# q and k of a head in transfers of 64 and 128 rows, and another order of ScalarE's queue before attention

## The chip, the cores and the metric

The kernel runs on one core of one Trainium2 chip. A core has four engines that compute, each with its own in-order queue: TensorE (PE in the profile, with its weight loads as PEld), VectorE (DVE), ScalarE (ACT) and GpSimd (POOL). A fifth, SyncE (SP), does nothing here but issue transfers. Transfers run on 16 DMA engines beside all of them. ACT and POOL issue some transfers too, and an engine that waits with an issue also holds up what stands behind it in its queue.

The metric is the device time of one execution in microseconds. The kernel before took 2428.34 us, the median of three runs (2427.61 to 2428.85).

## The reference

One decoder layer on x of 4096 x 1024, in float32: an RMS norm, an input projection, two groups of heads, gates, an output projection and a second norm.

```python
h = rms_norm(x, norm_gain)
qa, ka, va, ga, qr, kr, vr, gr = split(h @ w_in)
attn = dilated_attention(qa, ka, va)   # 8 heads of 64, branches (128,1), (512,4), (2048,16)
ret = retention(qr, kr, vr)            # 4 heads, key 64, value 128, chunks of 128
x = x + concat(silu(ga) * attn, silu(gr) * ret * ret_gn_gain) @ w_out
return rms_norm(x, final_gain)
```

Each attention head looks at its keys three times, with stride 1, 4 and 16, and merges the three results by their softmax denominators. q and k are rotated by their positions first.

## The kernel before, in words

It has three phases. **Phase 1** goes through x in eight blocks of 512 positions. For each block PE computes the projections in groups: q0, q1, k0, k1 (four heads of attention each), r0, r1 (retention's q and k), then the values. Every product is split in three matmuls (`mm3`) of high and low parts. A group gives two PSUM banks, A and B; there are seven such banks (`p1mm`). `rotate` turns them on DVE into two tiles `o` (tag `o`, two buffers), ACT and DVE split each into a tile `hl` (two buffers), and SP stores it to the DRAM tensors `dr["q"]`, `dr["k"]` or `dr["r"]`. In `dr["q"]` and `dr["k"]`, of shape [2, 2, 8, 32, 4096], the first index says whether the row is a high or a low part, the second which half of the 64 dimensions it belongs to, the third is the head. `store_values` scales a value bank on ACT into `vo` (two buffers) and ACT issues six transfers of it to `dr["v"]`, where the values lie in three orders, one for each stride.

In the last block the order is r0, r1, q0, q1, k0, k1. After r1 the function `make_room` loads the first head's q for its first 2048 positions (`load_q`, half 0). After k0, and before k1 is rotated, SP gets the load of x's first chunk of 128 positions (`load_x_chunk`) and the load of the first head's k but for the last 512 positions (`load_k`); after k1's rotation the rest of k. Then ACT's queue holds, in this order: the split of the first x chunk (`split_h_chunk`, ACT copies and POOL subtracts), eight splits of the weights w2 (`ahead["w2"].split`), and four times `store_values`. SP's queue has the load of the second x chunk after the second k load; it uses the same buffer as the first.

**Phase 2** is attention, with the retention and its values as filler. PE's order is fixed by hand: each head has 24 groups of four blocks of 128 queries, two steps a group, so 384 steps in all. Every step issues scores (`qk_bank`), transposes, products with v (`pv_group`) and copies of the results; between them the generator `filler` puts pieces of the retention, so many that a planned number of ns is filled. `LEAD` is the filler that comes before the first step. The groups of a head come in the order: stride 1 in the first half of the positions (4 groups), stride 4 (8), stride 16 (8), stride 1 in the second half (4). `gather_q` copies q of the strided groups together four steps ahead, part 0 on POOL and part 1 on DVE.

q lies in four tiles per head: high or low part (i), and first or second half of the positions. Each holds its 64 rows twice, in rows 0 to 63 and 64 to 127. k lies in one tile of 128 rows per head, in two pools that alternate. A head's k is loaded in the head before, from its group 6 on, its first half of q from group 20 on, its second half when the head begins. These loads go through a list, `pending`; `issue_due` sends of it at every step as many as a number `room` allows. Tiles of results have three buffers (`p2os`), their stores are issued two steps after the copy. v comes in tiles of 1024 positions, six buffers, two tiles ahead.

**Phase 3** has the gates, the output projection and the last norm, and is not touched.

Two lines that the steps below refer to: the cos and sin tables of phase 1 are loaded into 128 rows from 32 (L181), and rotated r is stored with the heads as the outermost index (L249):

```python
nc.sync.dma_start(tab[:, i, :], io[nm][:, b * BLK : (b + 1) * BLK].unsqueeze(0).broadcast_to([4, 32, BLK]))
nc.sync.dma_start(dr["r"][idx, :, part, :, cols], o)
```

Of the kernel before, what the change touches and what calls it, by code (L numbers as in the profile page):

```python
# [8 lines left out]
F32 = mybir.dt.float32  # L9
# [19 lines left out]
BLK = 512  # L29
NBLK = S // BLK  # L30
# [85 lines left out]
def phase1(tc, io, dr, right, ahead):  # L116
# [3 lines left out]
    nc = tc.nc  # L120
    gain, rs = ahead["gain"], ahead["rs"]
    with ExitStack() as ctx:
# [5 lines left out]
        op = ctx.enter_context(tc.tile_pool(name="p1o", bufs=2))  # L128
# [16 lines left out]
        for g in ("r", "k", "q", "v"):  # L145
            p = {"v": wp, "q": wpool}.get(g) or right.open(f"p1w{g}")
            i = "qkrv".index(g)
# [6 lines left out]
                tag="w" if g == "q" else None,  # L154
                room=[(qp[0], "q00"), (qp[0], "q10")] if g == "r" else None,
# [22 lines left out]
        def load_tables(b, n):  # L178
            tab = tp.tile([128, 2, BLK], F32, tag=f"tab{n}", name=f"tab{n}1")
            for i, nm in enumerate((f"cos{n}", f"sin{n}")):  # L180
                nc.sync.dma_start(tab[:, i, :], io[nm][:, b * BLK : (b + 1) * BLK].unsqueeze(0).broadcast_to([4, 32, BLK]))  # L181
            return tab
# [33 lines left out]
        def scaled(tab, rb):  # L216
            for i in range(2):
                nc.gpsimd.tensor_tensor(tab[:, i, :], tab[:, i, :], rb, ALU.mult)

        def products(g, i, hs, p, ks=range(KT)):  # L220

            for k in ks:
                mm3(
                    nc,
                    p,
                    [(*W[g].at(k, slice(i * 128, i * 128 + 128)), hs[k][:, 0, :], hs[k][:, 1, :])],
                    k == 0,
                    k == KT - 1,
                )

        def bank():
            return pmm.tile([128, BLK], F32, tag="mm", name="mm1")
# [34 lines left out]

        def store_values(b, i, p):
            n = 4 * b + i
            vf = op.tile([128, 512], F32, tag="vo", name="vo1")  # L270
            nc.scalar.activation(vf, p, AF.Copy, scale=rs[:, n : n + 1])

            nc.scalar.dma_start(dr["v"][0, n * 128 : (n + 1) * 128].rearrange("(r l) e -> l r e", r=16), vf)

            r0 = (n // 16) * 128 + (n % 16) * 8
            nc.scalar.dma_start(dr["v"][2].rearrange("(r q) e -> q r e", q=256)[r0 : r0 + 8], vf)

            for r in range(4):
                r0 = r * 1024 + b * 128 + i * 32
                nc.scalar.dma_start(dr["v"][1, r0 : r0 + 32].rearrange("(a l) e -> l a e", a=4), vf[r:128:4, :])  # L280
# [42 lines left out]
        for b in range(NBLK):  # L323
            last = b + 1 == NBLK
            names = "RA" if last else "AR"
            tabs = {"A": tabA, "R": tabR}
            if b:
                tabs[names[0]] = load_tables(b, names[0])
            xts, hnext, waiting = [], [], []
            for gi, (g, half) in enumerate(LASTG if last else GROUPS):  # L330
                if b == 0 and g == "q":
                    ps = first[2 * half : 2 * half + 2]
                else:
                    ps = [bank() for _ in range(2)]
                    for part in range(2):
                        products(g, 2 * half + part, hcur, ps[part])
                        if b and gi == 0 and part == 0:
                            diag = root(b)
                if gi == (0 if b else 2):
                    rb = along_free(b, diag)  # L340
                    scaled(tabs[names[0]], rb)
                    if b:
                        tabs[names[1]] = load_tables(b, names[1])
                        scaled(tabs[names[1]], rb)
                waiting.append((g, half, ps))

                while len(waiting) > 1 and rb is not None:
                    w, x, (A, B) = waiting.pop(0)
                    rotate(b, w, x, A, B, tabs["R" if w == "r" else "A"])
                if b == 0 and gi == 1:  # L350
                    for k in range(KT):
                        W["r"].split(k, nc.gpsimd if k % 2 else None)
                if b == 0 and gi == 3:
                    scaled(tabR, rb)
                    for k in range(KT):
                        W["v"].split(k, nc.gpsimd if k % 2 else None)
                if not last and gi >= 3:
                    while len(xts) < (2, 3, 4)[gi - 3]:
                        xts.append(load_xt(b + 1, len(xts)))
                    if gi == 4:  # L360
                        hnext.append(make_h(b + 1, 0, xts[0]))
                if last:
                    make_room(gi)
            if last:
                right.close(2)
                qp[1] = right.open("p2q1")
                hcp, kka = ahead["hcp"], ahead["kka"] = right.open("p2h"), right.open("p2ka")
                raw = load_x_chunk(nc, hcp, io, 0)
                kk = load_k(nc, kka, dr, 0, cols=slice(0, S - BLK))
                w, x, (A, B) = waiting.pop(0)  # L370
                rotate(b, w, x, A, B, tabs["A"])
                ahead["kk"] = load_k(nc, kka, dr, 0, cols=slice(S - BLK, S), t=kk)
                ahead["hch"] = {0: [split_h_chunk(nc, hcp, raw, 0, i) for i in range(2)]}
                ahead["hr"] = load_x_chunk(nc, hcp, io, 1)
                for k in range(KT):
                    ahead["w2"].split(k)
                for i in range(4):
                    p = bank()
                    for k in range(KT):
                        values(b, i, k, hcur, p)  # L380
                    store_values(b, i, p)
            else:
                pv = [bank() for _ in range(4)]
                for k in range(KT):
                    for i in range(4):
                        values(b, i, k, hcur, pv[i])
                    if k == 0:
                        w, x, (A, B) = waiting.pop(0)
                        rotate(b, w, x, A, B, tabs["R"])
                    if k + 1 < KT:  # L390
                        hnext.append(make_h(b + 1, k + 1, xts[k + 1]))
                    if len(xts) < KT:
                        xts.append(load_xt(b + 1, len(xts)))
                for i in range(4):
                    store_values(b, i, pv[i])
                hcur = hnext
# [22 lines left out]
def load_x_chunk(nc, pool, io, c):  # L419
    t = pool.tile([128, KT, 128], F32, tag="hr", name="hr2")  # L420
    nc.sync.dma_start(t, by_blocks(io["xT"])[:, :, c * 128 : (c + 1) * 128])
    return t


def split_h_chunk(nc, pool, t, c, i):

    hc = pool.tile([128, KT // 2, 2, 128], F32R, tag=f"hc{(2 * c + i) % 3}", name="hc2")
    src = t[:, KT // 2 * i : KT // 2 * (i + 1), :]
    nc.scalar.activation(hc[:, :, 0, :], src, AF.Copy)  # L429
    nc.gpsimd.tensor_tensor(hc[:, :, 1, :], src, hc[:, :, 0, :].bitcast(F32), ALU.subtract)  # L430
    return hc


def load_k(nc, pool, dr, h, dma=None, cols=slice(0, S), t=None):
    dma = dma or nc.sync.dma_start
    t = t or pool.tile([128, S], F32R, tag="kk", name="kk2")
    for i in range(2):
        for part in range(2):
            p0 = i * 64 + part * 32
            dma(t[p0 : p0 + 32, cols].bitcast(F32), dr["k"][i, part, h, :, cols])  # L440
    return t


# [61 lines left out]
def load_q(nc, pool, dr, h, i, half, dma=None):  # L505
    dma = dma or nc.sync.dma_start
    t = pool[half].tile([128, S // 2], F32R, tag=f"q{i}{half}", name=f"q2_{i}{half}")
    for dup in range(2):
        for part in range(2):
            p0 = dup * 64 + part * 32  # L510
            dma(t[p0 : p0 + 32, :].bitcast(F32), dr["q"][i, part, h, :, half * 2048 : (half + 1) * 2048])
    return t


def phase2(tc, io, dr, right, ahead, early3, raw, M):

    nc = tc.nc
    W2, hcp, kka, qp = (ahead[n] for n in ("w2", "hcp", "kka", "qp"))
    with ExitStack() as ctx:
# [47 lines left out]
        def issue_due():  # L567
            for fn, args in delayed.pop(clock[0], []):
                fn(*args)
            room = 250  # L570
            while pending and room > 0:
                dst, src = pending.pop(0)
                nc.sync.dma_start(dst, src)
                room -= dst.shape[0] * dst.shape[1] // 512

        pending = []

# [275 lines left out]
        hch, hraw = ahead["hch"], {1: ahead["hr"]}  # L853
# [555 lines left out]
```

## Time and profile before

| what | us |
|---|---|
| median of the three runs | 2428.34 |
| the profiled execution | 2426.76 |
| its span, first to last instruction | 2425.0 |
| phase 1 up to PE's last matmul before its hole | 761.86 |
| that hole of PE | 22.37 |
| attention's scores, first to last | 789.3 to 1657.0 |

In the profile's rows a line number follows the engine; `dst<-src` names tiles and tensors. SPq and ACTq are issues of transfers, not the transfers themselves; `[14.45 <-DMA x]` behind a row is the engine's idle time before it and what ended it. Issues of transfers in between are not counted as work, so an idle time on ACT can hold six of them. A row of windows has the length, then each engine's busy time with its number of instructions, the granted TensorE clock, the share of the 16 DMA engines' time that was busy, and the GB/s they moved. In the chain of work that ended last, a DMA row's length is the time from issue to landing.

### The profile page before, as it was taken

What the parts mean: (1) busy time and instruction counts of PE and PEld (TensorE: products, weight loads), DVE (VectorE), ACT (ScalarE), POOL (GpSimd) and SP (SyncE); (2) the same over time, 40 slices, a digit from 0 to 9 for tenths busy, and PEclk for the clock granted to TensorE, in tenths of its full rate; (3) what the DMA queues carried; (4) which work ended last, traced back from release to release, by engine and by line L of the source; (5) the groups of instructions that cost most, each with busy time, mean ns of one, the idle gap of its engine ahead of it and who ended that gap; (6) DMA issues with size and microseconds to landing.
All of it is one profiled execution on the core that took longest, in us unless ns stands there. A gap on an engine that the chain in (4) does not pass through costs nothing.

```text
span 2425.0 us, 41805 instructions
## 1 busy us (share of the span) xinstructions
PE 2339.9 (96%) x14568; PEld 1984.7 (82%) x14568; DVE 1486.3 (61%) x3921; ACT 992.1 (41%) x2868; POOL 721.8 (30%) x761
## 2 busy tenths in 40 slices
PE   7999999999996999999999999996899999999998
PEld 5778888888885888888888888875789999999997
DVE  5643543543432878787887879786655565565554
ACT  4322212212202666667666666666222232222221
POOL 5312112112112535353543535444221121121110
PEclk9999999999998999999999999998999999999999
DMA  6343343343356665757575665745665656666563
GB/s 191 130 144 112 127 143 114 125 143 123 118 161 187 163 162 138 182 130 192 130 178 150 164 157 135 181 137 169 154 159 166 142 159 163 144 164 156 141 155 92
DMA packets 404259, 362.59 MB, mean 150 GB/s; under 512 B 191848, under 2 KB 334824, under 8 KB 398928
## 3 DMA queue, kind: packets, MB, share of 16 engines
q1 hardware_dynamic: 389408, 332.91, 51.6%
q10 hardware_dynamic: 14112, 25.43, 3.4%
q8 instruction: 115, 1.88, 0.3%
q0 software_dynamic: 528, 1.58, 0.2%
q14 instruction: 96, 0.79, 0.1%
HBM read 241.18 MB, written 118.64 MB: 148 GB/s over the span
## 4 chain that ended last, share of the span: by engine, by line
PE 81%; DMA 6%; DVE 4%; ACT 2%; issue 1%; POOL 1%; ACTq 1%; SPq 1%; POOLq 0%; DVEq 0%
PE S L640 9%; PE O L710 7%; PE mm L50 7%; PE mm L49 7%; PE mm L51 7%; PE T L677 6%; PE po L50 4%; PE po L51 4%; PE po L49 4%; PE g L50 4%; PE g L49 4%; PE g L51 4%; PE V L49 3%; PE V L51 2%; PE V L50 2%; DMA wb<-dr_w 1%
## 5 line engine op out<-in xcount | busy, mean ns | idle before, releaser
L661 DVE CUSTOM_DVE_ANT_0 S<-S,mask 128x256 f32<-128x256 f32 (+1 forms) x768 | 308.4, 402 | 154.4 <-PE S L640 115.7
L668 ACT ACTIVATE P<-S,nm 128x256 f32<-128x256 f32 (+1 forms) x768 | 337.3, 449 | 44.4 <-DVE nm L661 41.1
L51 PE MATMUL g<-h,wg 128*128 128x256 f32 x1024 | 290.4, 284 | 0.0
L677 PE MATMUL T<-ident,P 128*128 128x128 f32 x1368 | 213.1, 273 | 0.5 <-ACT P L668 0.4
L50 PE MATMUL po<-wo,m 128*128 128x512 f32 x512 | 201.5, 394 | 0.0
L51 PEld LDWEIGHTS g<-h,wg 128*128 128x128 f32 x1024 | 197.5, 193 | 0.1
L710 PE MATMUL O<-pt,v 128*64 128x128 f32 (+1 forms) x1968 | 196.1, 325 | 0.2 <-ACT pt L687 0.2
L640 PE MATMUL S<-kk,qc 128*128 128x256 f32 x1024 | 186.5, 305 | 5.7 <-issue 2.6
L1202 POOL TENSOR_TENSOR rs<-v,mhalf 128x1 f32<-128x1 f32 x32 | 17.3, 540 | 554.5 <-DVE v L1200 554.5
L640 PEld LDWEIGHTS S<-kk,qc 128*128 128x128 f32 x1024 | 149.2, 190 | 33.5 <-issue 17.0
L51 PE MATMUL po<-wohi,m 128*128 128x512 f32 x448 | 176.3, 394 | 0.0
L49 PE MATMUL po<-wohi,m 128*128 128x512 f32 x448 | 174.8, 390 | 0.9 <-DVE x L1195 0.9
L173 POOL TENSOR_TENSOR sq<-sq,sq 128x512 f32<-128x512 f32 x56 | 76.3, 1362 | 331.4 <-ACT sq L169 331.4
L430 POOL TENSOR_TENSOR hc<-hr,hc 128x512 fp32r<-128x512 f32 x64 | 85.9, 1344 | 293.7 <-ACT hc L429 210.7
L710 PEld LDWEIGHTS O<-pt,v 128*64 128x64 f32 x1968 | 121.3, 136 | 60.7 <-issue 31.5
L677 PEld LDWEIGHTS T<-ident,P 128*128 128x128 f32 x1368 | 163.6, 141 | 1.1 <-ACT P L668 1.1
L49 PE MATMUL g<-h,wg1hi 128*128 128x256 f32 x512 | 146.0, 286 | 13.7 <-ACT h L464 13.7
L668 ACT ACTIVATION_READ_ACCUMULATOR P<-S,nm 128x1 f32 x768 | 157.5, 205 | 0.0
L41 ACT ACTIVATE m<-e 128x256 fp32r<-128x256 f32 x128 | 53.3, 417 | 240.8 <-DVE e L1148 140.9
L50 PE MATMUL g<-h,wg1hi 128*128 128x256 f32 x512 | 148.1, 289 | 3.8 <-DVE h L465 3.3
L49 PE MATMUL g<-h,wg0hi 128*128 128x256 f32 x512 | 145.0, 283 | 4.7 <-ACT e L1141 4.7
L1141 ACT ACTIVATE e<-g 128x256 f32<-128x256 f32 x128 | 48.3, 378 | 237.1 <-PE g L51 233.4
(207 smaller groups left out, 6207.5 us busy)
## 6 DMA issues: line engine op xcount, KB each, us to landing
q<-dr_q SPq DMA_DIRECT2D x128, 256.0 KB
hr<-in_xT_dram SPq DMA_DIRECT2D x64, 512.0 KB
wb<-dr_w SPq DMA_DIRECT2D x128, 192.0 KB
o<-dr_o SPq DMA_DIRECT2D x192, 128.0 KB
v<-dr_v SPq DMA_DIRECT2D x94, 256.0 KB
xt<-in_xT_dram SPq DMA_DIRECT2D x64, 256.0 KB
dr_q<-hl SPq DMA_DIRECT2D x32, 512.0 KB
dr_k<-hl SPq DMA_DIRECT2D x32, 512.0 KB
```

The lines of the kernel that those rows point to most:

```text
L41: nc.scalar.activation(dst[:, 0], src, AF.Copy)
L49: nc.tensor.matmul(out, wh, xh, start=first and i == 0, stop=False)
L50: nc.tensor.matmul(out, wh, xl, start=False, stop=False)
L51: nc.tensor.matmul(out, wl, xh, start=False, stop=last and i == n - 1)
L173: nc.gpsimd.tensor_tensor(sums[b], sums[b], sq, ALU.add)
L430: nc.gpsimd.tensor_tensor(hc[:, :, 1, :], src, hc[:, :, 0, :].bitcast(F32), ALU.subtract)
L640: nc.tensor.matmul(s[:, j * 256 : (j + 1) * 256], qq[h, t, half][:, off : off + 128] if br == 0 else it["q"][:, t, i, :], rhs, start=(j == ...
L661: nc.vector.tensor_tensor_reduce(sv, sv, mask[:, it["br"], c0:256], 1.0, BIG, ALU.add, ALU.min, accum_out=nm[:, col : col + 1])
L668: nc.scalar.activation(it["P", i // 2][:, i % 2, c0:256], sv, AF.Exp, bias=nm[:, col : col + 1], scale=-1.0, accum_out=den[:, col : col + 1])
L677: nc.tensor.transpose(t[:, j * 128 : (j + 1) * 128], it["P", bank][:, j // 2, j % 2 * 128 : j % 2 * 128 + 128], ident)
L710: nc.tensor.matmul(o[64 * bank : 64 * bank + 64, c0 : c0 + 128 * m], vt[h, br, idx // 8][:, idx % 8, :], it["pt"][:, a : a + m, :].rearran ...
L1141: nc.scalar.activation(e, g, AF.Silu)
```

## The change

Three things. `load_k` issues one transfer of 128 rows instead of four of 32, and `load_q` two transfers of 64 rows per tile instead of four of 32; the number that `issue_due` takes off `room` for a transfer is halved per element to fit. At the passage the first x chunk is split, and the second loaded, after the first of the last block's four `store_values` and no longer before the w2 splits. And the third and fourth of these `store_values` take a buffer of the tag `hl` instead of `vo`.

```diff
         def store_values(b, i, p):
             n = 4 * b + i
-            vf = op.tile([128, 512], F32, tag="vo", name="vo1")
+            if b + 1 == NBLK and i >= 2:
+                vf = op.tile([128, 2, BLK], F32, tag="hl", name="vo1")[:, 0, :]
+            else:
+                vf = op.tile([128, 512], F32, tag="vo", name="vo1")
             nc.scalar.activation(vf, p, AF.Copy, scale=rs[:, n : n + 1])
...
                 ahead["kk"] = load_k(nc, kka, dr, 0, cols=slice(S - BLK, S), t=kk)
-                ahead["hch"] = {0: [split_h_chunk(nc, hcp, raw, 0, i) for i in range(2)]}
-                ahead["hr"] = load_x_chunk(nc, hcp, io, 1)
                 for k in range(KT):
                     ahead["w2"].split(k)
                 for i in range(4):
@@
                         values(b, i, k, hcur, p)
                     store_values(b, i, p)
+                    if i == 0:
+                        ahead["hch"] = {0: [split_h_chunk(nc, hcp, raw, 0, j) for j in range(2)]}
+                        ahead["hr"] = load_x_chunk(nc, hcp, io, 1)
...
 def load_k(nc, pool, dr, h, dma=None, cols=slice(0, S), t=None):
     dma = dma or nc.sync.dma_start
     t = t or pool.tile([128, S], F32R, tag="kk", name="kk2")
-    for i in range(2):
-        for part in range(2):
-            p0 = i * 64 + part * 32
-            dma(t[p0 : p0 + 32, cols].bitcast(F32), dr["k"][i, part, h, :, cols])
+    dma(t[:, cols].bitcast(F32), dr["k"][:, :, h, :, cols].rearrange("i t d s -> (i t) d s"))
     return t
...
     for dup in range(2):
-        for part in range(2):
-            p0 = dup * 64 + part * 32
-            dma(t[p0 : p0 + 32, :].bitcast(F32), dr["q"][i, part, h, :, half * 2048 : (half + 1) * 2048])
+        p0 = dup * 64
+        dma(t[p0 : p0 + 64, :].bitcast(F32), dr["q"][i, :, h, :, half * 2048 : (half + 1) * 2048])
     return t
...
                 nc.sync.dma_start(dst, src)
-                room -= dst.shape[0] * dst.shape[1] // 512
+                room -= dst.shape[0] * dst.shape[1] // 1024
```

## The prediction, made before the changed kernel was run

> **What bounds the kernel now.** I read the page first, for the busy shares, the queues and the issues:
>
> ```profile
> PE 2339.9 (96%) x14568; PEld 1984.7 (82%) x14568; DVE 1486.3 (61%) x3921; ACT 992.1 (41%) x2868; POOL 721.8 (30%) x761
> ...
> q1 hardware_dynamic: 389408, 332.91, 51.6%
> ...
> q<-dr_q SPq DMA_DIRECT2D x128, 256.0 KB
> ...
> kk<-dr_k SPq DMA_DIRECT2D x28, 512.0 KB
> ```
>
> PE is busy for 96% of the span. The transfers fill half of the DMA engines' time, so they cost nothing as long as each lands before its reader. The change is about them and about one hole, so I read the windows of attention, of the passage to it and of the 3.4 us behind it:
>
> ```profile
> 790.00:1660.00 870.00, 858.81 (x6744) 719.41 (x6742) 698.48 (x2572) 600.58 (x2063) 401.41 (x450) 1.00 0.64 156
> 762.00:784.20 22.20, 0.00 (x0) 0.00 (x0) 0.87 (x3) 2.60 (x5) 3.85 (x6) 0.61 0.68 234
> 784.20:787.60 3.40, 3.37 (x10) 2.65 (x11) 0.00 (x0) 0.50 (x1) 3.33 (x4) 0.51 0.04 11
> ```
>
> The columns are length, busy time of PE, PEld, DVE, ACT and POOL, granted clock, DMA share, GB/s. In attention PE is busy for 858.8 of 870 us at full clock. At the passage it does nothing for 22.2 us and then runs 3.4 us at a clock of 0.51: a long hole costs 3.4 x 0.5 = 1.7 us more. The timeline of PE and ACT names the hole's end:
>
> ```profile
> 743.01 1.15 ACT L429 ACTIVATE hc<-hr 128x512 fp32r<-128x512 f32 x2 [3.27 <-DMA hr<-in_xT_dram]
> 744.07 4.39 ACT L84 ACTIVATE w2hi<-w,gain_all 128x512 fp32r<-128x512 f32 x7
> ...
> 767.84 0.69 ACT L271 ACTIVATE vo<-mm,rs_all 128x512 f32<-128x512 f32 x1 [4.75 <-DMA dr_v<-vo]
> ...
> 774.69 4.78 ACTq L280 DMA_DIRECT2D dr_v<-vo  x4
> 782.97 0.63 ACT L429 ACTIVATE hc<-hr 128x512 fp32r<-128x512 f32 x1 [14.45 <-DMA dr_v<-vo]
> 783.51 0.67 ACT L1009 ACTIVATE vch<-V,rs_all 128x512 f32<-128x512 f32 x1
> ...
> 784.23 0.80 PE L49 MATMUL V<-w2hi,hc 128*128 128x512 f32 x1 [22.37 <-ACT vch L1009]
> ```
>
> PE waits for vch, which stands in ACT's queue behind the last v store's transfers and a split (hc) that needs the second chunk of x.
>
> **How many engines a transfer runs on.** This decides the case. Two SP rows and six windows, in which hardly anything but the transfer named was in flight:
>
> ```profile
> 686.68 0.55 SPq L181 DMA_DIRECT2D tabA<-in_cosA_dram  x1
> ...
> 703.11 1.56 SPq L249 DMA_DIRECT2D dr_r<-o  x2
> ...
> 666.00:669.00 3.00, 3.00 (x14) 2.45 (x13) 0.00 (x0) 0.00 (x0) 0.00 (x0) 1.00 0.47 124
> 688.00:691.40 3.40, 3.40 (x16) 2.78 (x15) 2.84 (x6) 0.00 (x0) 0.95 (x1) 1.00 0.23 73
> 710.20:712.30 2.10, 2.10 (x11) 1.71 (x10) 0.00 (x0) 0.00 (x0) 0.00 (x0) 1.00 0.26 101
> 720.00:729.00 9.00, 9.00 (x40) 7.29 (x40) 6.74 (x11) 1.27 (x2) 0.00 (x0) 1.00 1.01 335
> 744.80:748.40 3.60, 3.60 (x18) 2.98 (x17) 3.28 (x4) 3.60 (x7) 1.92 (x2) 1.00 0.20 50
> 794.00:801.00 7.00, 7.00 (x56) 5.77 (x55) 5.92 (x24) 5.14 (x16) 3.54 (x4) 1.00 1.00 213
> ```
>
> A share of 1.00 is 16 engines. At 720 to 729 the w2 loads run (128 rows on both sides): all 16. At 794 to 801 the q loads of today (32 rows on both sides): all 16, though at 213 GB/s, not 335. At 666 to 669 the v stores, whose DRAM side is cut into 8 outermost pieces (L273 to L280): 0.47, about 8 engines. At 710 to 712 only the dr_r stores of L249, whose DRAM side has 4 heads outermost: 0.26, 4 engines. At 688 to 691 only the tabA loads, whose source is broadcast with 4 copies outermost (L181): 0.23, again 4. So a transfer uses as many engines as its outermost count on either side allows. The new k load has 4 pieces outermost ((i t) d s): 4 engines. The new q load has 2 (part, d, s): 2 engines. No row shows a 2; that it gives 2 continues 16, 8, 4.
>
> The Trainium skill, "DMA: Bandwidth & Descriptors", section "Why a DMA increments its semaphore by 16 and not by 1", says that a transfer's engines are the largest number up to 16 that divides the slowest dimension of both patterns; by it q gets 2 and k 4, and the sum is the one below. By that rule the 8 and the 4 of the windows agree; what it says of a 2 no run here shows yet, and four engines for q stay a rival.
>
> Rate of one engine, GB/s over 16 x share: 24.3 (dr_r), 19.8 (tabA), 15.6 (744.8 to 748.4, the tail of the kk loads on some three engines), 13.3 (q today). I take 17.7, the mean of the two rows that load SBUF with few engines; the ends are 24.3 and 13.3.
> - q transfer: 64 x 8 KB = 524,288 bytes, half on each engine: 262,144 / 17.7 = **14.8 us** (10.8; 19.7). Today 256 KB at 213 GB/s take 1.2.
> - k load: 128 x 16 KB, a quarter each: 524,288 / 17.7 = **29.6 us** (21.6; 39.4).
>
> **The change part by part.** Rows for the time there is:
>
> ```profile
> 790.63 3.70 SPq L573 DMA_DIRECT2D q<-dr_q  x8
> 803.86 1.50 POOL L616 CAST qc<-q 128x512 fp32r<-128x512 f32 x1
> ...
> 1092.46 2.78 SPq L573 DMA_DIRECT2D q<-dr_q  x6
> 1128.27 0.64 DVE L616 CAST qc<-q 128x512 fp32r<-128x512 f32 x1 [0.19 <-DMA q<-dr_q]
> 1092.40:1128.20 35.80, 35.60 (x290) 30.10 (x286) 26.37 (x101) 25.47 (x88) 11.73 (x13) 1.00 0.86 209
> ...
> L640 PE MATMUL S<-kk,q x512: 274/281/392, 789.3 to 1657.0; 128*128 128x256 f32 x171
> ...
> 718.20 4.26 DMA dr_q<-hl
> ```
>
> *q, from one head to the next.* The next head's first half is loaded from 1092.46 on, its second half from 1113, and the gather at 1128.27 needs the second: 36 us, already 0.19 us late. The second half's tiles are read by the old head's last groups, so the two halves come one after the other, and all eight transfers use the same two engines: 8 x 14.8 = 118. Beside it the other transfers' share of these engines: 0.86 x 35.8 = 30.8 us less 4.19 MB of q at 213 GB/s = 19.7 leaves 11. One hand-over, from issue to landing with little in front, is 4 (4.26 us). So 118 + 11 + 4 - 36 = **+97** (65; 137); nothing hides it, since PE has no idle time to give. Seven times: +680 (455; 959). For the first head the second half alone: 4 x 14.8 + 4 - 13 (790.63 to 803.86) = **+50** (34; 70).
>
> *k.* A step of attention is 867.7 us / 384 = 2.26. The k load goes out some 2 steps before the next store of O. O has three buffers, and one is wanted again 4 steps after its store's issue: 6 x 2.26 = 13.6 us after the k load. The store's part on the four engines stands behind k: 29.6 + 4 - 13.6 = **+20** each (12; 30), ACT waiting first and PE behind it. Seven times +140 (84; 210).
>
> *room // 1024.* Still two q transfers a step, but of twice the bytes, and one k. It sends them at most two steps (4.5 us) sooner into engines that are behind already: nothing.
>
> *The passage.* Rows:
>
> ```profile
> 693.38 10.72 DMA q<-dr_q
> 704.16 10.71 DMA dr_r<-o
> 712.49 0.69 DVE L241 TENSOR_TENSOR o<-mm,tabA 128x512 f32<-128x512 f32 x1 [8.80 <-DMA dr_r<-o]
> 734.48 0.39 PE L49 MATMUL mm<-w1vhi,h 128*128 128x512 f32 x1
> 733.33 1.56 SPq L260 DMA_DIRECT2D dr_k<-hl  x2
> 735.54 20.62 SPq L440 DMA_DIRECT2D kk<-dr_k  x4
> ```
>
> The first head's q loads stand in front of the last dr_r stores: today one such store takes 10.71 us instead of the 2.6 that 256 KB need at 101 GB/s, and q's rotation waits for it. Now 4 x 14.8 = 59 us from about 698, then two stores of 2.7: landed at 763 instead of 712.4, **+51**. PE holds 7 PSUM banks, stops before the second bank of the last k group (734.48 - 24 x 0.233 = 728.9) and goes on 37 us later. The k stores move from 733.3 to 784, landing at 786; the first k load (448 KB an engine) takes 26, its tail and hand-over 6, the second chunk of x stands behind it on these engines: about 820, and vch 822 instead of 783.5: **+38** (15; 68, with 10.8 and 19.7).
>
> ACT's new order puts the eight w2 splits before the hc splits: they need not wait until 743.01, 744.8 instead of 749.1 for the first v store; the two hc copies (1.15 us) and the load of the next chunk on SP follow that store. SP's own order stays (the second k load, then the chunk), POOL's subtraction has nothing queued behind it but the constants. The hl buffers for the third and fourth chunk free them of the earlier v stores; they wait for the last k stores instead, and behind them on ACT stand their transfers, hc and vch. With k that late this gains and costs nothing; without the q and k loads it would be worth 15 us (next part).
>
> *Clock.* Three holes a head and two at the passage, 23 x 1.7 = +39.
>
> Sum: 680 + 50 + 140 + 38 + 39 = **+947** (+627; +1346). The profiled execution took 2426.76 us, span 2425.0; the median shown is 1.6 above it. 2428 + 947 = **3375**; with the ends 3055 and 3775.
>
> **The rivals.**
> - *Sixteen engines all the same* (faster). If the count that matters were the rows in SBUF, the loads would get quicker (toward 335 GB/s) and only the passage would move: vch follows the fourth v store. The first comes at 744.8, each holds ACT for some 5.4 us (its 0.7 and six issues, 4.7 in the row of 767.84), hc takes 1.2 in between and 0.6 at the end: vch at 768 instead of 783.5, -15, **2412**. For it: today's 32-row loads get 213 GB/s where 128 rows get 335. Against it: 0.23 for tabA, whose SBUF side has 128 rows. It decides if the q loads' share of the DMA is 1. The Trainium skill, "DMA: Bandwidth & Descriptors", section "Rules for kernel authors", advises one 128-partition transfer in place of two on halves, and read alone that speaks for this rival; the trace doesn't bear it out for tabA, a 128-partition transfer on a quarter of the engines.
> - *Four engines for q too.* 7.4 us a transfer: 7 x (59 + 11 + 4 - 36 = 38) + 21 + 140 + 8 + 39 = +474: **2900**. Against it: 16, 8 and 4 follow the count.
> - *The two q engines hinder each other* and get 13.3 (today's 32-row loads run at that, the 128-row loads at 335 / 16.2 = 20.7, so rows close together seem to slow each other): **3775**. *They run undisturbed* at 24.3: **3055**. The rows of few engines lie between.
>
> **How the numbers follow.** The forecast (3200 to 3570) 0.45; undisturbed (3050 to 3200) 0.20; hindered (3570 to 3780) 0.13, above it 0.03; four engines 0.08; something in between the old time and 2850, 0.03; sixteen engines 0.08, of which 0.07 faster and 0.01 no change. The range 2880 to 3780 holds 0.86. A measurement of this kernel tells about 0.2% (5 us) from no change. Faster 0.07, same 0.01, slower 0.92.
>
> **What would show it.** Right: a DMA share near 0.13 while q alone is in flight; PE holes twice a head, ended by DVE or POOL L616 or by L640 on q; ACT L725 waiting behind kk; q's rotation near 763. Wrong: a share near 1 during q; heads still 108 us apart; the hole at the passage shorter and nothing else moved. If the heads are long but the waits end on v or O, the queue is the cause and not the engines' rate.

## The result, and the profile after

The changed kernel takes 3128.66 us, the median of four runs (3119.44 to 3135.69); the kernel before took 2428.6 beside it. The ratio is 1.288, with a 95% interval from 1.284 to 1.292. The forecast was 3375, its range 2880 to 3780: slower by 700 us where 947 were expected. The measured time lies in the band that the prediction gave to its rival "undisturbed" (3050 to 3200, chance 0.20), below the one of the forecast itself (3200 to 3570, 0.45). The profiled execution took 3131.73 us, its span 3129.9.

The page of the kernel after, busy shares, the main queue and the chain of work that ended last:

```profile
PE 2403.2 (77%) x14568; PEld 2029.4 (65%) x14568; DVE 1483.6 (47%) x3921; ACT 992.7 (32%) x2868; POOL 718.3 (23%) x761
...
q1 hardware_dynamic: 386948, 332.90, 37.4%
...
PE 55%; DMA 30%; SPq 6%; issue 2%; DVE 2%; ACT 1%; POOL 1%; ACTq 0%; POOLq 0%; DVEq 0%
DMA q<-dr_q 17%; DMA dr_o<-os 6%; PE mm L49 6%; PE mm L50 6%; PE mm L51 6%; PE S L640 5%; PE O L710 4%; PE po L50 4%; PE po L51 3%; PE po L49 3%; PE g L50 3%; PE g L51 3%; PE g L49 3%; PE T L677 3%; DMA hr<-in_xT_dram 2%
```

The bytes are the same 333 MB, and PE's share fell from 96% to 77%. The chain names two transfers: q, the loads that were changed, and the stores of O, which were not.

Windows of the kernel after (columns as before: length, busy time of PE, PEld, DVE, ACT and POOL, clock, DMA share, GB/s), and below them attention from the first scores to the last in the kernel before:

```profile
830.80:2362.30 1531.50, 914.35 (x6728) 758.06 (x6727) 695.82 (x2565) 598.64 (x2054) 396.48 (x450) 0.79 0.32 89
1000.00:1010.00 10.00, 0.00 (x0) 0.00 (x0) 0.00 (x0) 0.00 (x0) 0.00 (x0) 0.50 0.13 52
780.00:799.00 19.00, 0.00 (x0) 0.00 (x0) 0.39 (x2) 0.00 (x0) 0.00 (x0) 0.50 0.27 85
1220.60:1226.00 5.40, 5.31 (x26) 4.30 (x27) 1.67 (x6) 2.73 (x10) 1.27 (x1) 0.50 0.74 190
```

```profile
789.30:1657.00 867.70, 856.97 (x6729) 718.29 (x6728) 695.95 (x2565) 598.09 (x2054) 401.41 (x450) 1.00 0.64 157
```

The first row is attention from the first scores to the last: 1531.5 us where it took 867.7. PE's busy time grew from 857.0 to 914.4, so 57 us are matmuls at the lower clock, as in the fourth row (0.50 behind a hole). The rest of the 664 us is idle time. The second row has only q in flight: a share of 0.13 is 2.1 of 16 engines. The third has the first head's k and a little of a v store: 0.27, 4.3 engines. The landings in the trace say the same: beside one update at its issue, a load of q has two updates of its semaphore when it lands, a load of k four, and a store of O sixteen, one for each engine that carries a part of it.

PE's timeline over one head of the kernel after, the rows behind its holes; the idle time and its releaser stand in brackets:

```profile
1024.09 1.22 PE L640 MATMUL S<-kk,q 128*128 128x256 f32 x4 [29.81 <-ACT P L668]
...
1080.24 1.20 PE L640 MATMUL S<-kk,qc 128*128 128x256 f32 x4 [33.55 <-ACT P L668]
...
1127.01 1.19 PE L640 MATMUL S<-kk,qc 128*128 128x256 f32 x4 [17.27 <-ACT P L668]
...
1200.53 0.55 PE L640 MATMUL S<-kk,q 128*128 128x256 f32 x1 [7.85 <-DMA q<-dr_q]
1220.69 0.98 PE L640 MATMUL S<-kk,q 128*128 128x256 f32 x3 [19.61 <-DMA q<-dr_q]
```

A head has three holes: one at its start, on the first half of q (29.8; in the next head 7.9 and 19.6, with one of the four score products between them); one 56 us later (33.6), in front of the strided scores; and one of 17.3. Where the row says "ACT P", the last semaphore event was an old one: the engine named had long been done, and the wait was for data. The waits of the three engines that read the transfers tell which (us in total, times, longest):

```profile
ACT os L725 <- DMA dr_o<-os: 394.5, 14, 36.0
...
DVE qc L616 <- DMA q<-dr_q: 276.9, 8, 37.6
...
PE S L640 <- DMA q<-dr_q: 161.3, 11, 19.9
```

DVE's gather (qc) is held by q eight times, once a head: the second hole. PE itself waits for q at the heads' start. ACT's copy of O waits for the stores of earlier results: the third hole. The latter needs three views, SP's timeline, the chain (start, time from issue to landing) and ACT's timeline:

```profile
1283.23 0.59 SPq L573 DMA_DIRECT2D kk<-dr_k  x1
```

```profile
1286.90 32.73 DMA dr_o<-os
```

```profile
1319.73 0.38 ACT L725 ACTIVATE os<-O 128x256 f32<-128x256 f32 x1 [21.25 <-DMA dr_o<-os]
```

The store of 64 KB goes out 3.7 us behind k and takes 32.73 us, until 1319.6; ACT goes on at 1319.73. In the trace twelve of the store's sixteen updates have come 2.04 us after its issue. The last four come at 1314.9, 1316.5, 1318.5 and 1319.6, each 0.4 us behind one of k's four (1314.5, 1316.2, 1318.2, 1319.3).

Added up from the trace, PE's idle stretches of over 5 us in attention: the first head's second half 33; the seven other heads' holes on q 434, or 62 a head; the seven holes on k 141. With the 57 us of clock that is 665, all of the 664 but for rounding.

The passage, in ACT's, SP's and DVE's timelines of the kernel after:

```profile
777.50 26.19 ACTq L283 DMA_DIRECT2D dr_v<-vo  x4
803.74 1.15 ACT L433 ACTIVATE hc<-hr 128x512 fp32r<-128x512 f32 x2 [27.52 <-DMA dr_v<-vo]
...
823.92 0.69 ACT L1009 ACTIVATE vch<-V,rs_all 128x512 f32<-128x512 f32 x1 [5.31 <-DMA dr_v<-vo]
```

```profile
766.68 1.03 SPq L441 DMA_DIRECT2D kk<-dr_k  x1
```

```profile
744.65 0.69 DVE L241 TENSOR_TENSOR o<-mm,tabA 128x512 f32<-128x512 f32 x1 [43.99 <-DMA dr_r<-o]
```

q's rotation starts at 744.65 where it was 712.49; ACT stands in the middle of its first v store's issues for 26 us while k is in flight. In the trace SP and ACT use eight semaphores in turn for their transfers; ACT's issue that takes the semaphore of the first k load again starts at 800.62, and that load lands at 800.60. vch comes at 823.92 instead of 783.5, and the first scores at 830.8 instead of 789.3: +41.5. Behind attention nothing moved.

### The profile page after: what moved, and what is told of

It reads as the page before. It is cut to its first block, busy times and chain, and to the rows that moved or that the text cites. A ratio compares the mean times of both kernels' runs of the same rounds, so it can differ in the third digit from the quotient of the medians.

```text
span 3129.9 us, 41667 instructions
## 1 busy us (share of the span) xinstructions
PE 2403.2 (77%) x14568; PEld 2029.4 (65%) x14568; DVE 1483.6 (47%) x3921; ACT 992.7 (32%) x2868; POOL 718.3 (23%) x761
## 4 chain that ended last, share of the span: by engine, by line
PE 55%; DMA 30%; SPq 6%; issue 2%; DVE 2%; ACT 1%; POOL 1%; ACTq 0%; POOLq 0%; DVEq 0%
DMA q<-dr_q 17%; DMA dr_o<-os 6%; PE mm L49 6%; PE mm L50 6%; PE mm L51 6%; PE S L640 5%; PE O L710 4%; PE po L50 4%; PE po L51 3%; PE po L49 3%; PE g L50 3%; PE g L51 3%; PE g L49 3%; PE T L677 3%; DMA hr<-in_xT_dram 2%
## 5 line engine op out<-in xcount | busy, mean ns | idle before, releaser
L640 PE MATMUL S<-kk,qc 128*128 128x256 f32 x1024 | 199.7, 321 | 412.7 <-ACT P L668 386.9
L725 ACT ACTIVATE os<-O 128x256 f32<-128x256 f32 x128 | 49.3, 385 | 658.0 <-DMA dr_o<-os 394.5
L640 PE MATMUL S<-kk,q 128*128 128x256 f32 x512 | 97.6, 313 | 204.3 <-DMA q<-dr_q 161.3
L677 PE MATMUL T<-ident,P 128*128 128x128 f32 x1368 | 227.5, 286 | 0.4 <-ACT P L668 0.4
L640 PEld LDWEIGHTS S<-kk,q 128*128 128x128 f32 x512 | 76.5, 200 | 221.7 <-issue 162.5
L710 PE MATMUL O<-pt,v 128*64 128x128 f32 (+1 forms) x1968 | 215.1, 348 | 0.2 <-ACT pt L687 0.2
L677 PEld LDWEIGHTS T<-ident,P 128*128 128x128 f32 x1368 | 175.1, 149 | 1.1 <-ACT P L668 1.1
L616 DVE CAST qc<-q 128x512 fp32r<-128x512 f32 x64 | 43.4, 679 | 276.9 <-DMA q<-dr_q 276.9
L49 PE MATMUL g<-h,wg1hi 128*128 128x256 f32 x512 | 146.9, 288 | 14.4 <-ACT h L465 14.4
L49 PE MATMUL V<-w2hi,hc 128*128 128x512 f32 x256 | 120.0, 469 | 39.9 <-ACT hc L433 28.2
```

The source lines that it names most:

```text
L49: nc.tensor.matmul(out, wh, xh, start=first and i == 0, stop=False)
L616: (nc.vector if part else nc.gpsimd).tensor_copy(t[:, part].rearrange("p b j -> p (b j)"), src)
L640: nc.tensor.matmul(s[:, j * 256 : (j + 1) * 256], qq[h, t, half][:, off : off + 128] if br == 0 else it["q"][:, t, i, :], rhs, start=(j == ...
L677: nc.tensor.transpose(t[:, j * 128 : (j + 1) * 128], it["P", bank][:, j // 2, j % 2 * 128 : j % 2 * 128 + 128], ident)
L710: nc.tensor.matmul(o[64 * bank : 64 * bank + 64, c0 : c0 + 128 * m], vt[h, br, idx // 8][:, idx % 8, :], it["pt"][:, a : a + m, :].rearran ...
L725: nc.scalar.activation(ob, it["O"][:, :256], AF.Copy)
```

## Experiments

### The order and the buffers alone

The changed kernel with the old loads:

```diff
-    dma(t[:, cols].bitcast(F32), dr["k"][:, :, h, :, cols].rearrange("i t d s -> (i t) d s"))
+    for i in range(2):
+        for part in range(2):
+            p0 = i * 64 + part * 32
+            dma(t[p0 : p0 + 32, cols].bitcast(F32), dr["k"][i, part, h, :, cols])
...
-        p0 = dup * 64
-        dma(t[p0 : p0 + 64, :].bitcast(F32), dr["q"][i, :, h, :, half * 2048 : (half + 1) * 2048])
+        for part in range(2):
+            p0 = dup * 64 + part * 32
+            dma(t[p0 : p0 + 32, :].bitcast(F32), dr["q"][i, part, h, :, half * 2048 : (half + 1) * 2048])
...
-                room -= dst.shape[0] * dst.shape[1] // 1024
+                room -= dst.shape[0] * dst.shape[1] // 512
```

> The changed kernel with q and k loaded as before, in 32-row transfers: only the order of ScalarE's queue at the passage and the two hl buffers stay. Theory (the loads' outermost count of 2 and 4 puts them on 2 and 4 DMA engines, and that alone makes the 700 us): heads 108 us apart again, PE's hole at the passage shorter than 22 us, about 2413 us. Rival (the passage itself does harm, the k stores' buffers make the values wait): 2430 us or more.

Measured 2429.61 beside 2432.09: a ratio of 0.9991 (0.9982 to 1.0001). Without the new loads the 700 us are gone. The order's own gain is less than can be told from nothing, where 15 us were expected; the first scores come 3.6 us earlier (785.7). ACT's timeline shows where the rest stayed:

```profile
745.03 0.70 ACT L274 ACTIVATE vo<-mm,rs_all 128x512 f32<-128x512 f32 x1
...
762.47 0.69 ACT L274 ACTIVATE vo<-mm,rs_all 128x512 f32<-128x512 f32 x1 [9.04 <-DMA dr_v<-vo]
773.18 0.69 ACT L274 ACTIVATE vo<-mm,rs_all 128x512 f32<-128x512 f32 x1 [10.03 <-DMA dr_v<-vo]
...
779.34 0.67 ACT L1013 ACTIVATE vch<-V,rs_all 128x512 f32<-128x512 f32 x1
```

The first v store starts at 745.0, as the rival's working had it (744.8), but the third and fourth start 9.7 and 10.7 us after the one before them, where 5.4 were taken, and vch comes at 779.3 and not at 768. Most of the idle time in front of these two rows are the six issues of the store before.

### Loads of 64 rows that keep 16 engines

Against the changed kernel the order of the rows is changed: d (32) is put ahead of the part, on the DRAM side, so that the outermost count is 32. k goes in two transfers of 64 rows, one for the high and one for the low parts, instead of one of 128. The scores are sums over those rows, and q and k are permuted alike.

```diff
-    dma(t[:, cols].bitcast(F32), dr["k"][:, :, h, :, cols].rearrange("i t d s -> (i t) d s"))
+    for i in range(2):
+        dma(t[64 * i : 64 * i + 64, cols].bitcast(F32), dr["k"][i, :, h, :, cols].rearrange("t d s -> d t s"))
...
-        dma(t[p0 : p0 + 64, :].bitcast(F32), dr["q"][i, :, h, :, half * 2048 : (half + 1) * 2048])
+        dma(
+            t[p0 : p0 + 64, :].bitcast(F32),
+            dr["q"][i, :, h, :, half * 2048 : (half + 1) * 2048].rearrange("t d s -> d t s"),
+        )
```

> The changed kernel with the rows of q and k in another order, (d, part) in place of (part, d), on both, so that their products stay the same: q goes in the same 64-row transfers of 512 KB, k in two of 64 rows, but the outermost count of the DRAM side is 32. Theory of the outermost count: 16 engines each, a DMA share near 1 while q alone is in flight, no holes at the heads, about the time of the kernel with the old loads (2405 to 2420 us). Rival (large transfers block the queue or its completion slots, whatever engines they use): at least 2800 us, since q's transfers have the same size and number.

Measured 2417.2 beside 2432.09: a ratio of 0.9941 (0.9929 to 0.9952), 15 us faster than the kernel before and over 700 faster than the changed one, with the same bytes, the same 64 rows and the same number of q transfers. Two windows, of q's loads in attention and of the hole at the passage, and the row behind that hole in PE's timeline:

```profile
781.00:784.00 3.00, 3.00 (x24) 2.72 (x23) 1.77 (x9) 1.60 (x5) 0.00 (x0) 1.00 1.02 235
762.50:771.50 9.00, 0.00 (x0) 0.00 (x0) 0.87 (x3) 1.36 (x3) 4.27 (x5) 0.67 0.70 237
```

```profile
772.09 0.79 PE L49 MATMUL V<-w2hi,hc 128*128 128x512 f32 x1 [10.22 <-ACT vch L1013]
```

All sixteen engines again (1.02, and sixteen updates at the landing of each load), so the size of a transfer is not what slowed it. Nor does it speed it up: 235 GB/s over everything in flight, against 213 with 32 rows. The hole at the passage is 10.2 us instead of 22.4, the first scores come at 777.4, and attention itself is about as long as before (868.6 against 867.7).

### The two loads, each alone

q in 64 rows with the old k, and k in 128 rows with the old q, both with the new order; each is one half of the first experiment's diff.

> The changed kernel with k loaded as before in four 32-row transfers; q stays in 64-row transfers of outermost count 2. Theory: the two holes a head that end on q stay (29 and 33 us in the changed kernel), the one behind k goes (20 us and 3.5 us of half clock, seven times): about 3129 - 165 = 2960 us, 2900 to 3000.

Measured 2967.64, within the theory's range.

> The changed kernel with q loaded as before in 32-row transfers; k stays in one 128-row transfer of outermost count 4. Theory: one hole a head of about 20 us, ended by a store of O behind k, and a little clock: 2413 + 165 = 2580 us, 2540 to 2620. Rival (k's hole in the changed kernel only came from q's backlog on the same engines): under 2480 us.

Measured 2604.32, within the theory's range and far above the rival's. Over the 2429.6 of the order alone that is 538 for q and 175 for k. Together they would give 3142; the changed kernel took 3129. So the two hardly touch one another. With k alone each head has one hole; in the window of attention PE is idle for 157 of 1031 us:

```profile
799.90:1831.30 1031.40, 874.18 (x6728) 729.87 (x6727) 698.21 (x2564) 597.25 (x2054) 400.50 (x450) 0.92 0.53 132
```

### q in smaller pieces on two engines

As the run of q alone, but each q load in two halves by columns: the same 256 KB as before the change, still two pieces outermost.

```diff
         p0 = dup * 64
-        dma(t[p0 : p0 + 64, :].bitcast(F32), dr["q"][i, :, h, :, half * 2048 : (half + 1) * 2048])
+        for c in range(2):
+            cs = slice(c * 1024, (c + 1) * 1024)
+            dma(t[p0 : p0 + 64, cs].bitcast(F32), dr["q"][i, :, h, :, half * 2048 : (half + 1) * 2048][:, :, cs])
```

> As e3 (k old), but each 64-row transfer of q is cut in two of 1024 columns, 256 KB each as in the kernel before, and as many of them; the outermost count is still 2. Theory (two engines carry all of q, at 26.7 GB/s each): the last of a tile's transfers lands as late as in e3, 2968 us within 30. Rival (one long transfer holds a completion slot and SP's queue for long): 256 KB transfers free the slots sooner, under 2850 us.

Measured 2925.0, 13 us below the theory's range and 75 above the rival's: transfers of the old size are nearly as slow as large ones, and the number of engines is what counts. The 43 us come from shorter holes: the first half's is 18 to 23 us in six of seven heads, where it was 20 to 30. That a group starts once its own piece is there would explain it; this was not tested.

### What holds PE while k is loaded: the queue or the engines

As k alone, with k in attention issued by ACT, and then by POOL, whose transfers have a queue of their own.

```diff
         def soon(dst, src):
-            pending.append((dst, src))
+            pending.append((dst, src, nc.sync.dma_start))
+        def soon_act(dst, src):
+            pending.append((dst, src, nc.scalar.dma_start))    # second kernel: nc.gpsimd
...
-                dst, src = pending.pop(0)
-                nc.sync.dma_start(dst, src)
+                dst, src, dma = pending.pop(0)
+                dma(dst, src)
...
-                            kk[h + 1] = load_k(nc, kkb if h % 2 == 0 else kka, dr, h + 1, soon)
+                            kk[h + 1] = load_k(nc, kkb if h % 2 == 0 else kka, dr, h + 1, soon_act)
```

> As e4 (q old, k in one 128-row transfer of outermost count 4), but in attention the k transfers are issued by ScalarE instead of SP. Theory (the stores of O stand behind k in SP's queue on the four engines, and that makes the hole of 20 us): from another queue k no longer stands in front of them; holes of under 6 us, 2604 - 7 x 17 = 2485 us, 2440 to 2520. Rival (the four engines are simply too busy with k, from whichever queue): 2570 us or more.

Measured 2587.73, 17 us less than with SP; 119 less had been expected. SP still stopped for some 30 us in most heads, which suggested the slots that the next expectation speaks of: a slot is one of the eight semaphores that SP's and ACT's transfers use in turn.

> The kernel with only k in 128 rows, with k of the heads in attention issued by GpSimd, whose transfers have completion slots of their own. Two theories of the 17 to 26 us hole per head. Slots: SP and ScalarE share eight completion slots, used in turn; k holds one for its 35 us, the eighth transfer after it needs that one again, and SP's queue stops there until k has landed (28.5 us inside a group of stores of O in the run with k on SP, 30 us without an issue in the run with k on ScalarE). Then SP no longer stops, the stores of O go out, and the time is 2430 to 2470. Engines: the stores of O and the loads of v themselves queue behind k on its four DMA engines; then the hole stays and the time is 2570 or more, as with k on ScalarE.

Measured 2598.2. The hole is there with every issuer: 2604, 2588 and 2598. The waits of ACT's copies of O, first with k on ACT and then with k on POOL (total, times, longest; with k on SP they are 158.3, 7, 27.5):

```profile
ACT os L730 <- DMA dr_o<-os: 147.9, 11, 24.5
```

```profile
ACT os L730 <- DMA dr_o<-os: 147.8, 10, 25.5
```

And one of them in the kernel with k on POOL, in the timelines of POOL, SP and ACT:

```profile
953.99 0.78 POOL L574 DMA_DIRECT2D kk<-dr_k  x1
```

```profile
959.46 29.61 SPq L747 DMA_DIRECT2D dr_o<-os  x4
989.12 0.58 SPq L594 DMA_DIRECT2D v<-dr_v  x1
```

```profile
992.00 0.38 ACT L730 ACTIVATE os<-O 128x256 f32<-128x256 f32 x1 [21.32 <-DMA dr_o<-os]
```

SP issues four stores in 29.6 us although no k stands in its queue or holds a slot of its own. The theory of the slots therefore falls as the cause of the hole, and so does the one of a single queue: the hole stays when k goes through another.

What the landings show is not the same for every issuer. The stores of O that go out within 6 us behind k have twelve of their sixteen updates after 2 to 4 us in all four kernels. With k on SP, in the changed kernel and in k alone, the last four come 0.2 to 1.0 us behind k's four, for all 28 such stores (30 to 38 us from issue to landing): their parts stand behind k, as the prediction said. With k on ACT or POOL the last four come between 27 us before k's and 1.2 us behind them, 11 to 36 us after the issue. In one head with k on POOL four such stores land 12.7, 18.6, 23.7 and 28.2 us after k's issue, some 5 us apart. So from another queue a store does not have to wait for all of k, but it is slow on k's four engines. This looks like taking turns on them; that was not tested. The holes stay: PE's idle stretches of over 5 us in attention add up to 147, 112 and 125 us with k on SP, ACT and POOL.

SP's issues come to a stop in two ways. In the changed kernel and with k alone on SP or ACT, the transfer that takes k's slot again starts within 0.1 us behind k's landing in every head, so that wait is for k. With k on SP or POOL, SP also stands for 20 to 29 us of most heads in the issue of one store; what this waits for was not settled. With k on SP neither stop is needed for the hole: the store that ACT waits for in the result's rows goes out 3.7 us behind k, before SP stops. With k on ACT or POOL it is open how much of the hole is due to them.

### q and k issued by POOL

The changed kernel, with `load_q` and `load_k` in attention sent to POOL by the same few lines.

> The changed kernel with q and k of the heads in attention issued by GpSimd. If q is late because its two engines are slow, the holes that end on q stay: 2925 to 3000, the time of q in 64 rows alone, with k's part gone if slots are its cause, and 3100 or more if engines are. If q is late because SP's queue stops at the slots that q and k hold, q comes earlier and the time falls below 2850. In both cases the waits of ScalarE's os for stores of O (394.5 us in the changed kernel) fall, if they are of SP's queue.

Measured 2834.2, 294 us less than with SP and 91 below the lower end for slow engines. So for q the issuer does count. Waits of PE and ACT, and a window with six q loads in flight:

```profile
ACT os L729 <- DMA dr_o<-os: 165.3, 12, 25.8
...
PE S L644 <- DMA q<-dr_q: 107.2, 14, 17.9
```

```profile
975.50:980.00 4.50, 0.00 (x0) 0.00 (x0) 0.00 (x0) 1.41 (x5) 0.00 (x0) 0.99 0.80 179
```

The wait for stores falls from 394.5 to 165.3, about what k alone leaves (148 to 158). But two things differ from the loads on SP, and the expectation had only one of them. The second half of q is issued earlier: in two pairs, 14 and 41 us after the first half (973.77 and 1000.63 against 959.51); on SP the same head's comes 57 us after it (1029.70 against 973.17). And the loads no longer share two engines: in the window shown q's packets fill 10.8 engines and move 155 GB/s. A load from POOL has sixteen updates in the trace; of those of the six loads issued between 959.51 and 974.45, 2, 4, 6, 8, 10 and 12 come only after 985, as if each load added two engines of its own to those that are busy. One load takes longer, 22 to 27 us, but they run side by side: the first half has landed 32 us after its first issue, on SP after 48. So the run cannot tell slow engines from a stopped queue, since it changes both; how much of the 294 us is due to either stays open.

### The loads alone, in the old order

> The kernel before with only the changed loads (64 and 128 rows, outermost counts 2 and 4) and the new room; the order of ScalarE's queue and the v buffers are those of before. Theory (with q and k that late the passage's order gains and costs next to nothing): 3129 us within 15. Rival (the new order makes part of the loss, as the third and fourth v store wait for late k stores): under 3110 us.

This is the kernel before with the change's three hunks in `load_k`, `load_q` and `issue_due`. Measured 3143.23, one run, beside 3128.7 with the new order, whose four runs spread over 16 us; the first scores come at 840.7 instead of 830.8. So the order costs nothing here; by the first scores it gains some 10 us, which a single run cannot confirm.

### Sixteen engines in the old order, and without the two buffers

The loads with d outermost in the kernel before:

> The kernel before (its order of ScalarE's queue, its v buffers), with q and k in 64-row transfers of outermost count 32, rows in the order (d, part). It tells what the new order is worth once the loads are quick. Theory A (the new order and the loads help each other: e2's first score came 12 us earlier than before, the order alone gave 3.6): 2422 to 2432 us, within 0.3% of before. Theory B (the passage gains from fewer and quicker k transfers alone, the order does nothing): 2417 us, as e2.

Measured 2425.61 beside 2430.59: 0.9977 (0.9966 to 0.9988). The loads alone gain 0.2%, the order alone 0.1% or nothing, both together 0.6%: each has its full effect only with the other.

The loads with d outermost and the new order, without the two `hl` buffers for v:

```diff
-            if b + 1 == NBLK and i >= 2:
-                vf = op.tile([128, 2, BLK], F32, tag="hl", name="vo1")[:, 0, :]
-            else:
-                vf = op.tile([128, 512], F32, tag="vo", name="vo1")
+            vf = op.tile([128, 512], F32, tag="vo", name="vo1")
```

> The kernel with rows of q and k taken in the order (d, part), without the two more buffers for v; the order of ScalarE's queue as changed. If the two buffers carry a part of the 14 us by which that kernel is under the kernel before, the third store of v waits for its buffer again and the first product of attention is 5 to 10 us later: 2422 to 2427. If they carry nothing: 2415 to 2419.

Measured 2417.64 beside 2433.32: 0.9931 (0.9913 to 0.9948), the same as with the buffers. They carry nothing there; the order and the loads do. What the two together free shows in SP's timeline, of the order alone and then of the order with the new loads:

```profile
736.19 17.55 SPq L444 DMA_DIRECT2D kk<-dr_k  x4
753.84 5.37 SPq L260 DMA_DIRECT2D dr_k<-hl  x2
```

```profile
735.53 1.74 SPq L442 DMA_DIRECT2D kk<-dr_k  x2
742.60 8.09 SPq L260 DMA_DIRECT2D dr_k<-hl  x2
```

With four k loads SP is held 17.6 us at its issues, and the last k stores stand behind them; with two loads it is free after 1.7, and those stores start 11 us earlier. That this is what lets the v stores through is read from the order of the rows and was not tried by itself.

## Why the prediction was right, and what was mis-sized

**How many engines.** Right. q alone in flight shows a share of 0.13 and k 0.27, so 2 and 4, and the same rows with 32 outermost run on all sixteen. The updates at the landings, two for a load of q and four for k, say the same. The rule of the Trainium skill ("DMA: Bandwidth & Descriptors", section "Why a DMA increments its semaphore by 16 and not by 1") holds here for 2 as well, which no row before showed. With it fall the rivals of four engines for q and of sixteen all the same. The Trainium skill's section "Rules for kernel authors" on that page, from which the prediction took the advice of one 128-partition transfer, also says that an outermost dimension of fewer than 16 pieces confines a transfer to at most that many engines; read together, the section did not speak for sixteen.

**q at the heads, +680: the mis-sized term.** The step was right (eight loads one after the other, and two holes a head), the rate was not. I took 17.7 GB/s for one engine, the mean of two rows; alone in flight the two engines moved 52 GB/s, 26 each, above the upper end of 24.3. That is 262,144 / 26 = 10.1 us a transfer and not 14.8, and in the same sum 8 x 10.1 + 11 + 4 - 36 = 60 us a head. Measured: 434 / 7 = 62. The rival "run undisturbed" had the rate almost right; the one in which the two engines hinder each other (13.3) falls. The first head's second half, +50, came to 33 for the same reason. Both together: 467 instead of 730, the whole of the error and a little more.

**k, +140.** Right in its mechanism: in every head the last four updates of the stores come just behind k's four. In size it came to 141, but by two errors that nearly cancel. k took 34 to 38 us and not the 29.6 taken; but PE also ran on for longer before it needed the buffer (36 - 20 = 16 us, where 13.6 less a hand-over of 4 were taken). Besides, SP's issues stop while k is in flight, which the prediction did not have.

**The clock, +39.** Right in kind, short in size: 57 in attention alone. The 1.7 us were taken from one hole of 22 us, with 3.4 us at half clock behind it. In attention of the kernel after, the trace's record of the clock has 22 stretches at 0.50 that begin in holes, and PE is busy in them for 5.0 us on average (3.5 to 6.7), 5.4 in the row shown.

**The passage, +38.** It came to +41.5, against 38 and two holes' clock of 1.7, but by two errors that cancel. With the faster engines q's rotation started at 744.65 and not at 763, and k's load went out at 766.68 and not near 786. But behind k's landing, at 800.6 in the trace, three of the four v stores were still to come, since ACT was stuck in the issues of the first for 26 us, at the slot that k held; the prediction had only the chunk of x behind k. vch came at 823.92, against 822.

**The rival of sixteen engines, 2412.** It did not happen here, but its price can be seen: with loads that do keep the sixteen engines the gain is 15 us, as it had. Its working was wrong on one point: it gave the 15 us to the order alone, and the order alone gives hardly any of them.

## What to carry to other kernels

Before transfers are merged, look at the outermost count of both sides: a merged load that leaves 2 or 4 pieces outermost runs on that many engines. Every later transfer of the same queue with a part on these engines lands behind it, and those of another queue are slow there too. Here it was enough to put the dimension of 32 ahead of the one of 2 to turn a loss of 29% into a gain of 0.6%. And when a wait is priced, take the rate from a row in which as few engines are busy as will be, not from a mean over rows that share them.

## What was not expected of the hardware

- With two engines busy, each moved 26 GB/s; with some four it was 85 / (16 x 0.27) = 20, with 16 on 64 rows 235 / (16 x 1.02) = 14. So two engines do a quarter of the work of sixteen, not an eighth.
- 64 rows on sixteen engines were hardly quicker than 32 (235 and 213 GB/s, with other transfers in both).
- A load of 2 MB on four engines held stores of 64 KB from the same queue for 30 to 38 us at a DMA share of 0.3, and those of another queue for 11 to 36 us. The next transfer on its semaphore, from SP or ACT, was not issued before it had landed.
- Loads of q from SP shared the same two engines, one after the other. Issued by POOL, each ran on two as well, as the updates read, but on two others than the load before it: six in flight filled 10.8 engines.
